# First expert's weight splits released by the last tile's logits, the routing slots and the first gathered rows

## The chip, the cores and the metric

The kernel runs on one core of one Trainium2 chip. The metric is the device time of one execution in microseconds (us); less is better. The engines of the core are named as the profile names them: PE is TensorE (matmuls), PEld its weight loads, DVE is VectorE, ACT is ScalarE, POOL is GpSimd and SP is SyncE, which here only issues transfers.

## The reference

The reference is a stack of four layers over 1024 tokens of width 1024. The change touches the feed-forward part of the first two layers, an expert-choice mixture with 16 experts:

```python
def expert_choice_ffn(xn, w_router, w_gate, w_up, w_down):
    cap = EC_CAPACITY_FACTOR * T // N_EXPERTS            # 128 tokens per expert
    aff = jax.nn.softmax((xn @ w_router).astype(jnp.float32), axis=-1)
    g, idx = lax.top_k(jnp.swapaxes(aff, 1, 2), cap)     # every expert picks its tokens
    xg = xn[bidx, idx]
    hid = jax.nn.silu(jnp.einsum('becd,edf->becf', xg, w_gate)) * jnp.einsum('becd,edf->becf', xg, w_up)
    y = jnp.einsum('becf,efd->becd', hid, w_down) * g[..., None].astype(xn.dtype)
    return jnp.zeros_like(xn).at[bidx, idx].add(y)
```

Here T is 1024, D is 1024 and the inner width is 768, so w_gate and w_up of one expert are 1024 x 768 and w_down is 768 x 1024.

## The kernel before

Every matmul in full precision is done in three products. An operand is split into a high part (rounded by ACT) and a low part (the rest, mostly by DVE), and high x low, low x high and high x high are added up on PE. So each weight that is loaded costs ACT one pass and DVE (or POOL) one pass before PE can use it.

The class `Moe` holds one feed-forward part. `mix_out` walks over eight tiles of 128 tokens: PE projects, `route_tile` adds the residual, normalizes, and makes the router's logits. ACT copies the logits out of PSUM as `lgs` (L1047), and for the last tile (t = 7) this is the last thing ACT has to do before the routing. `route` then finds each expert's 128 best tokens with a long row of small DVE instructions, and ends with `slot`: for each token its place in each expert's list. `slz` (L1165) is a column of zeros made from `slot`.

`experts` loops over the 16 experts. `fetch(e)` makes a one-hot map `oh` from `slot` on DVE (L1216), multiplies it on PE to get the list of token numbers (`idx`), casts it on DVE (L1223), sums the gains on DVE (`gsc`, L1231), and gathers the 128 rows `xg` with an indirect transfer that POOL issues (L1233). The map has one buffer, so the next expert's map waits for the matmuls of the one before. `tokens(e)` transposes the rows on PE (`xgT`) and splits them into `xgh` (ACT) and `xgl` (DVE); for the first expert in pieces of 128 x 256. The experts' `fetch(0)` and `fetch(1)` stand ahead of the loop, `fetch(e + 2)` and `tokens(e + 1)` inside it with raised priority.

`load` brings one unit of weights, 128 x 3072 (1536 KB): half of a gate, up or down matrix. SP issues it (L1186), and it is split in three stretches of 1024 columns. Units are counted in `self.units`: units 1 and 2 are the first expert's gate, 3 and 4 its up, 5 and 6 the second expert's gate, 7 and 8 its up, and then 9 and 10 the first expert's down (an expert's down follows the next expert's gate and up). Raw weights have four buffers for gate/up/down and two more, high and low parts have three buffers each; a load into a buffer waits for the low parts made from the unit that was in it.

Units 1 to 4 are loaded long before the routing ends. Units 1 to 3 are split by two lines of their own, L1195 and L1196: the high part adds `slz`, which is zero, as its bias, so that it waits for the slots. From unit 4 on, `K.split` (L130 on ACT, L134 on DVE or POOL) does it.

The order of instructions on each engine is fixed when the kernel is built: a planner runs through the kernel on a simulated timeline and puts an instruction on its engine's queue by priority and by the time at which its inputs are there. On the chip each engine then takes its queue strictly in order.

Of the kernel before, what the change touches and what calls it, by code (L numbers as in the profile page):

```python
# [10 lines left out]
F32 = mybir.dt.float32  # L11
# [3 lines left out]
AF = mybir.ActivationFunctionType  # L15
OP = mybir.AluOpType
# [4 lines left out]
P = 128  # L21
T = 1024
D = 1024
NT = T // P
KT = D // P
# [905 lines left out]
class Moe:  # L931
# [5 lines left out]
    def prepare(self, pool):  # L937
        K, nc, a = self.K, self.K.nc, self.K.a
        self.rt = pool.tile([P, KT, 32], F32, name="rt")
        nc.gpsimd.memset(self.rt, 0.0)  # L940
        nc.sync.dma_start(out=self.rt[:, :, 0:NE], in_=a["router_w"][self.layer].rearrange("(k p) e -> p k e", p=P))
        gc = K.small.tile([KT, P], F32, name="rgr", tag="colraw", bufs=2)
        nc.sync.dma_start(out=gc, in_=a["ffn_norm_g"][self.layer].rearrange("(k p) -> k p", p=P))
        gt = K.psum("rgt", "mm")
        K.transpose(gt[:, 0:KT], gc)
        nc.vector.tensor_tensor(out=self.rt[:, :, 0:NE], in0=gt[:, 0:KT].rearrange("p (k o) -> p k o", o=1).broadcast_to([P, KT, NE]),
                                in1=self.rt[:, :, 0:NE], op=OP.mult)
        self.aff = pool.tile([P, NT, NE], F32, name="aff")
        self.rhs = pool.tile([P, NT, NE, 5], BF16, name="lrhs")
        with K.pool("iot", 1) as ip:  # L950
            iot = ip.tile([P, 2, NT, NE], F32, name="iot")
            nc.gpsimd.iota(iot[:, 0], pattern=[[0, NT], [0, NE]], base=0, channel_multiplier=1, allow_small_or_imprecise_dtypes=True)
            nc.gpsimd.iota(iot[:, 1], pattern=[[P, NT], [0, NE]], base=0, channel_multiplier=0, allow_small_or_imprecise_dtypes=True)
            nc.gpsimd.tensor_copy(out=self.rhs[:, :, :, 0], in_=iot[:, 0])
            nc.gpsimd.tensor_copy(out=self.rhs[:, :, :, 4], in_=iot[:, 1])
        self.iota = pool.tile([P, P], F32, name="iotac")
        nc.gpsimd.iota(self.iota, pattern=[[1, P]], base=-1000, channel_multiplier=0, allow_small_or_imprecise_dtypes=True)
        self.affp = pool.tile([P, 4, 2, 2, 32], F32, name="affp")
        nc.gpsimd.memset(self.affp, 0.0)
# [53 lines left out]
    def route_tile(self, wk, h, t, project):  # L1013

        K, nc = self.K, self.K.nc
        V = nc.vector
        ts = slice(t * P, (t + 1) * P)
        cuts = (0, 512, 1024) if t == NT - 1 else (0, 1024)  # L1020
        xn = wk.tile([P, D], F32, name="xn", tag="xn")
        xt = wk.tile([P, D], F32, name="xnt", tag="xnt")
        n = len(cuts) - 1
        ss = self.sp.tile([P, n], F32, name="ss", tag=f"rss{n}", bufs=2)
        out, tp = K.psum("out"), K.psum("xnT", "tp")
        if t % 2 == 0:
            self.e = self.sp.tile([P, 2, NE], F32, name="re", tag="re", bufs=2)
        ps = K.psum("lg", "mm")
        for i, (c0, c1) in enumerate(zip(cuts, cuts[1:])):
            cs = slice(c0, c1)  # L1030
            project(out, c0, c1)
            V.tensor_tensor(out=h[:, cs], in0=out[:, cs], in1=h[:, cs], op=OP.add)
            K.norm_stats(h[:, cs], xn[:, cs], ss[:, i:i + 1])
            for k in range(c0 // P, c1 // P):
                K.transpose(tp[:, k * P:(k + 1) * P], h[:, k * P:(k + 1) * P])
            nc.scalar.activation(out=xt[:, cs], in_=tp[:, cs], func=AF.Copy)
            for k in range(c0 // P, c1 // P):
                j = k % 4 * 32
                K.mm(ps[j:j + 32, 0:P], self.rt[:, k], xt[:, k * P:(k + 1) * P], k < 4, k >= 4)
        nc.sync.dma_start(out=self.hD[ts, :], in_=h)  # L1040
        if n > 1:
            V.tensor_tensor(out=ss[:, 0:1], in0=ss[:, 0:1], in1=ss[:, 1:2], op=OP.add)
        ss = ss[:, 0:1]
        V.tensor_scalar(out=ss, in0=ss, scalar1=1.0 / D, scalar2=EPS, op0=OP.mult, op1=OP.add)
        rs = K.rsqrt(ss, 1)
        ls = self.sp.tile([P, P], F32, name="lgs", tag="lgs", bufs=2)
        nc.scalar.activation(out=ls, in_=ps[:, 0:P], func=AF.Copy)  # L1047
        K.transpose(ps[:, P:2 * P], ls)
        lg = self.sp.tile([P, NE], F32, name="lg", tag="lg", bufs=2)
        V.tensor_reduce(out=lg, in_=ps[:, P:2 * P].rearrange("p (j e) -> p e j", j=4)[:, 0:NE], axis=AX.X, op=OP.add)  # L1050
        mx = self.sp.tile([P, 1], F32, name="rmx", tag="rmx", bufs=2)
        V.tensor_reduce(out=mx, in_=lg, axis=AX.X, op=OP.max)
        V.tensor_scalar(out=self.e[:, t % 2], in0=lg, scalar1=mx, scalar2=rs, op0=OP.subtract, op1=OP.mult)
        if t % 2:
            self.affinities(t - 1)

        def normed():
            V.scalar_tensor_tensor(out=xn, in0=h, scalar=rs, in1=self.gb, op0=OP.mult, op1=OP.mult)
            nc.sync.dma_start(out=self.xnD[ts, :], in_=xn)

        if t < NT - 1:
            normed()
        else:
            self.normed = normed
# [63 lines left out]
    def route(self, pool):  # L1128

        K, nc, tc, a = self.K, self.K.nc, self.K.tc, self.K.a  # L1130
        V = nc.vector
        aff = self.aff
        with K.pool(name="rt", bufs=1, side="right") as rp:
# [18 lines left out]
            for t in range(NT):  # L1152
                lo, n = t + 1, NT - t
# [3 lines left out]
            slot = pool.tile([P, NT, NE], F32, name="slot")  # L1157
# [3 lines left out]
            V.scalar_tensor_tensor(out=tmp, in0=tmp, scalar=-1000.0, in1=sel[:, 0:NT, 1], op0=OP.add, op1=OP.mult)  # L1161
            V.tensor_tensor(out=slot, in0=slot, in1=tmp, op=OP.add)
            self.slot = slot
            self.zero = pool.tile([P, 1], F32, name="slz")
            V.tensor_scalar(out=self.zero, in0=slot[:, 0, 0:1], scalar1=0.0, scalar2=None, op0=OP.mult)  # L1165

            rhs = self.rhs
            res = rp.tile([P, NT, NE], F32, name="affr")
# [10 lines left out]
    def load(self, W, k0, n, c):  # L1179


        K, nc = self.K, self.K.nc
        kt = W.shape[0] // P
        r3 = self.raw(n, c, self.units % 6 > 3)
        raw = r3.rearrange("p k c -> p (k c)")
        nc.sync.dma_start(out=r3, in_=W.rearrange("(p k) c -> p k c", k=kt)[:, k0:k0 + n, :])  # L1186
        hi = self.wp.tile([P, 3072], F32R, name="mwh", tag="mwh", bufs=3)
        lo = self.wp.tile([P, 3072], F32R, name="mwl", tag="mwl", bufs=3)
        self.units += 1
        for j in range(3):  # L1190
            s = slice(j * 1024, (j + 1) * 1024)
            if self.units > 3:
                K.split(hi[:, s], lo[:, s], raw[:, s], lo_eng="pool" if self.units % 6 == 3 else "dve")
            else:
                nc.scalar.activation(out=hi[:, s], in_=raw[:, s], func=AF.Identity, bias=self.zero)  # L1195
                nc.vector.tensor_tensor(out=lo[:, s], in0=raw[:, s], in1=hi[:, s].bitcast(F32), op=OP.subtract)  # L1196
        return hi.rearrange("p (k c) -> p k c", k=n), lo.rearrange("p (k c) -> p k c", k=n)

    def accumulate(self, ps, parts, xh, xl, W, c):
# [48 lines left out]
    def experts(self, x0):  # L1248

        K, nc, a, L = self.K, self.K.nc, self.K.a, self.layer  # L1250
        V = nc.vector
        self.units, self.first = 0, []
        with K.pool("exw", 1) as self.wp, K.pool("exr2", 2) as self.rawp2, K.pool("ex", 2) as wk, K.pool("exx", 2, side="right") as xk:
            ahead = [self.fetch(wk, xk, 0), self.fetch(wk, xk, 1)]
            x = self.tokens(xk, ahead[0], 2)
            last = None
            for e in range(NE):
                idx, g, _ = ahead[e]
# [6 lines left out]
                for name in ("gate", "up"):  # L1265
# [3 lines left out]
                    if name == "gate" and e + 1 < NE:  # L1269
                        with K.first():  # L1270
                            x = self.tokens(xk, ahead[e + 1])
# [42 lines left out]
class Gqa:  # L1314
# [60 lines left out]
    def project(self, u, ws, wk, uh, ul, t):  # L1375

        K, nc = self.K, self.K.nc
        ts = slice(t * P, (t + 1) * P)
        ps = K.psum("qk")
        for j, (wh, wl) in enumerate(ws):  # L1380
            K.mm3(ps[:, j * 256:(j + 1) * 256], lambda k: uh[:, k, ts], lambda k: ul[:, k, ts], lambda k: wh[:, k], lambda k: wl[:, k], KT, n=256)
        if u == 1:
            p3 = ps[:, 0:256].rearrange("p (h d) -> p h d", h=4)
            K.split(self.v[:, t, :, 0:64], self.v[:, t, :, 64:128], p3)
            return
        x = self.rotated(wk, ps, u, t)
        tp = K.psum("qkT")
        for b in range(4):
            K.transpose(tp[:, b * P:(b + 1) * P], x[:, b * P:(b + 1) * P])
        tv = tp.rearrange("p (b t) -> p b t", b=4)  # L1390
        o, nq = (2, 4) if u else (0, 2)
        nc.scalar.activation(out=self.qT[:, o:o + nq, ts], in_=tv[:, 0:nq], func=AF.Copy, scale=0.125)
        if u == 0:
            nc.scalar.activation(out=self.kT[:, :, ts], in_=tv[:, 2:4], func=AF.Copy)
# [962 lines left out]
```

## Time and profile before

| what | value |
|---|---|
| time, median of 3 runs | 3875.89 us |
| lowest and highest | 3873.57, 3886.39 us |
| time of the profiled execution | 3871.14 us |
| its span | 3869.4 us |
| PE busy | 3548.5 us (92%) |
| DVE busy | 2800.8 us (72%) |
| ACT busy | 2089.2 us (54%) |
| POOL busy | 1068.8 us (28%) |

The span runs from the first to the last instruction of the profiled execution; its own time lies 1.7 us above. The slots are there at 932 us of the span in the first layer and at 2066 us in the second, and the expert loops follow. The places that the change touches are short: some 40 us from the last tile's logits to the second expert's first matmul, once in each layer, so they are read from the timeline of each engine and not from sums over the span.

### The profile page before, as it was taken

The page shows a single profiled execution, that of the slowest core. Times are in us where ns is not written, and L with a number is a line of the kernel's source. Part 1 is how long each engine was busy: PE and PEld are TensorE (multiplying, and loading weights), DVE is VectorE, ACT ScalarE, POOL GpSimd, SP SyncE. Part 2 cuts the span into 40 slices and gives each one's busy share as a digit, 9 for nine tenths or more (in the row PEclk, how much of TensorE's full clock was granted, in tenths as well). Part 3 has the DMA queues.
Part 4 walks back from the last instruction along what each step waited for, and adds up shares of the span by engine and source line. Part 5 has one row for each costly group of instructions (what it writes and reads, how often), then busy time and mean ns, then how long its engine had stood idle before and what let it go on. Part 6 is the DMA issues. An engine that isn't in the chain of part 4 may idle for free. (4 is left out here: it accounts for less than half of the span.)

```text
span 3869.4 us, 52797 instructions
## 1 busy us (share of the span) xinstructions
PE 3548.5 (92%) x19679; PEld 3015.0 (78%) x19679; DVE 2800.8 (72%) x4844; ACT 2089.2 (54%) x3234; POOL 1068.8 (28%) x939
## 2 busy tenths in 40 slices
PE   7997999985999989899895999989998999999998
PEld 6885878764988879877785988878876877778777
DVE  6547878857988779777777988776476866666565
ACT  4333432222776763689834776754486138665520
POOL 2004655400454321244401454322343000000010
PEclk9998999987999999999997999999999999999999
DMA  4223233354999961000265999961113312222441
GB/s 155 96 83 108 104 133 129 125 198 170 355 357 350 357 237 41 16 12 10 61 225 203 372 352 355 356 199 44 48 32 100 121 43 96 85 96 66 142 144 63
DMA packets 221321, 603.64 MB, mean 156 GB/s; under 512 B 23350, under 2 KB 129704, under 8 KB 195465
## 3 DMA queue, kind: packets, MB, share of 16 engines
q1 hardware_dynamic: 209369, 558.59, 40.2%
q0 software_dynamic: 11696, 41.69, 4.1%
q8 instruction: 155, 2.54, 0.3%
q14 instruction: 101, 0.83, 0.1%
HBM read 503.60 MB, written 96.60 MB: 155 GB/s over the span
## 5 line engine op out<-in xcount | busy, mean ns | idle before, releaser
L134 DVE TENSOR_TENSOR mwl<-mwr,mwh 128x1024 fp32r<-128x1024 f32 x468 | 612.7, 1360 | 67.4 <-ACT mwh L130 66.5
L130 ACT ACTIVATE mwh<-mwr 128x1024 fp32r<-128x1024 f32 x558 | 545.5, 1050 | 55.6 <-PE up L176 29.3
L134 POOL TENSOR_TENSOR mwl<-mwr,mwh 128x1024 fp32r<-128x1024 f32 x90 | 252.7, 2836 | 295.9 <-ACT mwh L130 277.3
L1864 POOL DMA_DIRECT2D pyr<-y3T_d x31 | 23.5, 758 | 723.0 <-PE z L176 592.6
L1233 POOL DMA_INDIRECT xg<-xn_d,idx x32 | 69.5, 2173 | 414.4 <-ACT mwh L1195 281.5
L915 POOL TENSOR_TENSOR oh<-oh,oh 64x256 f32<-64x256 f32 (+1 forms) x56 | 55.2, 985 | 396.9 <-ACT oh L914 382.4
L176 PE MATMUL gate<-mwh,xgl 128*128 128x384 f32 x512 | 140.2, 355 | 8.8 <-DVE xgl L134 8.8
L176 PE MATMUL gate<-mwl,xgh 128*128 128x384 f32 x512 | 138.4, 348 | 1.0 <-DVE mwl L134 0.7
L134 DVE TENSOR_TENSOR gpl<-pT,gph 128x512 fp32r<-128x512 f32 x168 | 110.5, 684 | 39.6 <-ACT gph L130 25.7
L873 DVE TENSOR_REDUCE mx<-gs 128x1 f32<-128x1024 f32 x96 | 116.9, 1217 | 30.4 <-PE gs L176 30.1
L125 PE MATMUL pT<-ident,prob 128*128 128x128 f32 x896 | 125.7, 275 | 13.9 <-DVE gpl L134 8.3
L125 PEld LDWEIGHTS pT<-ident,prob 128*128 128x128 f32 x896 | 104.5, 141 | 39.8 <-ACT prob L875 7.1
L176 PE MATMUL gate<-mwh,xgh 128*128 128x384 f32 x512 | 135.0, 344 | 0.0
L176 PE MATMUL up<-mwl,xgh 128*128 128x384 f32 x512 | 133.3, 340 | 1.8 <-DVE mwl L134 1.8
L176 PE MATMUL up<-mwh,xgh 128*128 128x384 f32 x512 | 133.5, 340 | 0.0
L176 PE MATMUL up<-mwh,xgl 128*128 128x384 f32 x512 | 132.8, 340 | 0.0
L176 PE MATMUL out<-pwh,pyl 128*128 128x512 f32 x384 | 121.8, 398 | 10.0 <-DVE pyl L134 10.0
L176 PE MATMUL down<-mwl,hh 128*128 128x512 f32 x384 | 123.5, 403 | 3.0 <-POOL mwl L134 2.7
L176 PE MATMUL down<-mwh,hl 128*128 128x512 f32 x384 | 122.8, 399 | 0.0
L176 PE MATMUL out<-pwl,pyh 128*128 128x512 f32 x384 | 121.7, 398 | 0.0
L176 PE MATMUL out<-pwh,pyh 128*128 128x512 f32 x384 | 121.6, 398 | 0.0
L176 PE MATMUL down<-mwh,hh 128*128 128x512 f32 x384 | 121.2, 396 | 0.0
(746 smaller groups left out, 11329.1 us busy)
## 6 DMA issues: line engine op xcount, KB each, us to landing
mwr<-in_exp_w_gate_dram SPq DMA_DIRECT2D x64, 1536.0 KB
mwr<-in_exp_w_up_dram SPq DMA_DIRECT2D x64, 1536.0 KB
mwr<-in_exp_w_down_dram SPq DMA_DIRECT2D x64, 1536.0 KB
raw<-in_ssd_w_in_dram SPq DMA_DIRECT2D x40, 512.0 KB
csr<-cs_d SPq DMA_DIRECT2D x32, 512.0 KB
k_d<-kev SPq DMA_DIRECT2D x54, 256.0 KB
kt<-k_d SPq DMA_DIRECT2D x54, 256.0 KB
raw<-in_hy_w_in_dram SPq DMA_DIRECT2D x10, 1024.0 KB
```

What stands on the lines that cost most here:

```text
L125: self.nc.tensor.transpose(out, in_, self.ident[:n, :n])
L130: nc.scalar.activation(out=hi, in_=src, func=AF.Copy)
L134: e.tensor_tensor(out=lo, in0=src, in1=hi.bitcast(F32), op=OP.subtract)
L176: self.nc.tensor.matmul(out=out, lhsT=lhsT, rhs=rhs, start=start, stop=stop)
L873: nc.vector.tensor_reduce(out=mx, in_=ps, axis=AX.X, op=OP.max, negate=True)
L915: nc.gpsimd.tensor_tensor(out=o2, in0=o2, in1=o, op=OP.add)
L1233: nc.gpsimd.indirect_dma_start(out=xg, out_offset=None, in_=self.xnD, in_offset=bass.IndirectOffsetOnAxis(ap=idx[:, 0:1], axis=0))
L1864: K.nc.gpsimd.dma_start(out=raw, in_=yT[q].rearrange("(p k) t -> p k t", k=self.kt)[:, :, t * P:(t + 1) * P])
```

## The change

The high parts of units 1 to 3 no longer take their zero from the slots. `route_tile` makes a new zero `lgz` on ACT from the last tile's `lgs`, and that is now the bias. The low parts of these units become a three-operand instruction on DVE, (raw + zero) - high, whose zero is a column: for unit 1 the zero from the slots, for units 2 and 3 a new zero `xgz`, which DVE makes from the last low part of the first expert's rows after `tokens` (whose last piece is written last). All these zeros have the value 0, so no result changes.

```diff
@@ prepare
         self.aff = pool.tile([P, NT, NE], F32, name="aff")
+        self.zero = pool.tile([P, 1], F32, name="lgz")
@@ route_tile
         nc.scalar.activation(out=ls, in_=ps[:, 0:P], func=AF.Copy)
+        if t == NT - 1:
+            nc.scalar.activation(out=self.zero, in_=ls[:, 0:1], func=AF.Copy, scale=0.0)
@@ route
-            self.zero = pool.tile([P, 1], F32, name="slz")
-            V.tensor_scalar(out=self.zero, in0=slot[:, 0, 0:1], scalar1=0.0, scalar2=None, op0=OP.mult)
+            self.late = [pool.tile([P, 1], F32, name=n) for n in ("slz", "xgz")]
+            V.tensor_scalar(out=self.late[0], in0=slot[:, 0, 0:1], scalar1=0.0, scalar2=None, op0=OP.mult)
@@ load
                 nc.scalar.activation(out=hi[:, s], in_=raw[:, s], func=AF.Identity, bias=self.zero)
-                nc.vector.tensor_tensor(out=lo[:, s], in0=raw[:, s], in1=hi[:, s].bitcast(F32), op=OP.subtract)
+                nc.vector.scalar_tensor_tensor(out=lo[:, s], in0=raw[:, s], scalar=self.late[self.units > 1], in1=hi[:, s].bitcast(F32), op0=OP.add, op1=OP.subtract)
@@ experts
             x = self.tokens(xk, ahead[0], 2)
+            V.tensor_scalar(out=self.late[1], in0=x[1][:, KT - 1, 0:1].bitcast(F32), scalar1=0.0, scalar2=None, op0=OP.mult)
```

## Rows read from the trace of the kernel before

**Rows 1.** Timeline of ACT, first layer: start, busy us, instruction, idle before and releaser

```profile
904.25 0.28 ACT L1047 ACTIVATE lgs<-lg 128x128 f32<-128x128 f32 x1 [0.61 <-PE lg L176]
914.50 0.56 ACT L1171 ACTIVATE lrhs<-aff 128x128 bf16<-128x128 f32 x1 [9.97 <-DVE aff L1078]
...
932.63 9.47 ACT L1195 ACTIVATE mwh<-mwr,slz 128x1024 fp32r<-128x1024 f32 x9 [15.45 <-DVE slz L1165]
942.06 0.38 ACT L130 ACTIVATE xgh<-xgT 128x256 fp32r<-128x256 f32 x1
```

**Rows 2.** Timeline of DVE, first layer, slots to first rows

```profile
932.44 0.15 DVE L1165 TENSOR_SCALAR slz<-slot 128x1 f32<-128x1 f32 x1
932.51 1.22 DVE L1216 TENSOR_TENSOR oh<-iotac,slot 128x1024 bf16<-128x1024 f32 x1
933.81 1.23 DVE L1196 TENSOR_TENSOR mwl<-mwr,mwh 128x1024 fp32r<-128x1024 f32 x1
934.95 0.15 DVE L1223 CAST idx<-idx 128x1 int32<-128x1 f32 x1
...
936.22 3.49 DVE L1196 TENSOR_TENSOR mwl<-mwr,mwh 128x1024 fp32r<-128x1024 f32 x3
...
940.76 0.15 DVE L1223 CAST idx<-idx 128x1 int32<-128x1 f32 x1
...
940.89 5.76 DVE L1196 TENSOR_TENSOR mwl<-mwr,mwh 128x1024 fp32r<-128x1024 f32 x5
946.57 1.63 DVE L134 TENSOR_TENSOR xgl<-xgT,xgh 128x256 fp32r<-128x256 f32 x4
```

**Rows 3.** Timeline of PE, first layer

```profile
936.36 0.58 PE L176 MATMUL idx<-lrhs,oh 128*128 128x4 bf16 x16 [1.99 <-DVE oh L1216]
940.88 1.94 PE L125 MATMUL xgT<-ident,xg 128*128 128x128 f32 x8 [3.94 <-DMA xg<-xn_d,idx]
947.04 1.01 PE L176 MATMUL gate<-mwh,xgl 128*128 128x384 f32 x2 [4.22 <-DVE xgl L134]
...
956.42 0.74 PE L125 MATMUL xgT<-ident,xg 128*128 128x128 f32 x4 [3.66 <-DMA xg<-xn_d,idx]
...
972.17 0.51 PE L176 MATMUL gate<-mwh,xgl 128*128 128x384 f32 x2
```

**Rows 4.** Timeline of POOL, first layer

```profile
936.06 1.32 POOL L1233 DMA_INDIRECT xg<-xn_d,idx  x1 [141.63 <-ACT mwh L1195]
941.20 6.31 POOL L1233 DMA_INDIRECT xg<-xn_d,idx  x1 [3.82 <-DVE gsc L1231]
```

**Rows 5.** Timeline of SP's queue, first layer

```profile
938.60 5.00 SPq L1186 DMA_DIRECT2D mwr<-in_exp_w_up_dram  x2
```

**Rows 6.** Stretches: PE, PEld, DVE, ACT, POOL busy (x), clock, DMA share, GB/s

```profile
956.90:960.20 3.30, 3.30 (x13) 3.30 (x13) 0.69 (x1) 0.60 (x1) 0.00 (x0) 0.50 0.25 94
...
972.00:977.00 5.00, 5.00 (x30) 5.00 (x30) 5.00 (x6) 3.44 (x5) 0.00 (x0) 1.00 0.89 317
957.50:965.00 7.50, 7.50 (x38) 7.50 (x38) 3.75 (x4) 4.44 (x6) 0.00 (x0) 0.81 0.04 15
```

**Rows 7.** Instructions of L1058, all: min/median/max ns

```profile
L1058 DVE SCALAR_TENSOR_TENSOR xn<-hres,rs_y,ffn_gb x16: 1266/1278/1285, 819.5 to 2040.1; 128x1024 f32<-128x1024 f32 x16
```

**Rows 8.** Transfers by queue, 953 to 956 us: packets, MB, share

```profile
q0 software_dynamic: 107, 0.37, 41.1%
q1 hardware_dynamic: 50, 0.44, 34.8%
```

**Rows 9.** Transfers by queue, 941 to 944 us

```profile
q1 hardware_dynamic: 83, 1.02, 91.1%
```

**Rows 10.** Timeline of PE, second layer

```profile
2080.26 1.01 PE L176 MATMUL gate<-mwh,xgl 128*128 128x384 f32 x2 [4.58 <-DVE xgl L134]
...
2105.58 0.51 PE L176 MATMUL gate<-mwh,xgl 128*128 128x384 f32 x2
...
2247.02 0.93 PE L125 MATMUL hT<-ident,hid 128*128 128x128 f32 x3 [2.10 <-DVE xgl L134]
```

## Prediction

> **What bounds the kernel now.** The page gives PE 92% of the span, so a change is worth something only where PE stands still or runs at its lower clock. I read the timeline of ACT first, then DVE, PE, POOL and SP around the slots, then stretches for the clock, then the same places in the second layer.
>
> ACT copies the last logits at 904.25, does nothing until 914.50, and after short copies waits 15.45 us for the zero from the slots; only then does it make nine high parts in 9.47 us [rows 1]. DVE is the engine that ends last here: after the slots it has three one-hot maps of 1.22 us, nine low parts at some 1.16 us each, and the casts between them, without a pause until 946.57 [rows 2]. The first expert's rows are on the chip at 940.88, when PE transposes them, but the first low part of the rows is made at 946.57, behind five low parts of weights, and the first gate matmul starts at 947.04 after PE has stood 4.22 us [rows 2, 3]. So the weights' low parts, needed later, sit in front of the rows' low parts, needed first.
>
> A second stop follows: PE waits 3.66 us until 956.42 for the second expert's rows [rows 3]. That gather is issued late (941.20), since its cast comes at 940.76 although its matmuls, begun at 936.36, take 0.58 us; and POOL needs 6.31 us for it where the first took 1.32 [rows 2 to 4]. After the stop PE's granted clock is 0.50, the 1.2 GHz level, for some 3.3 us; later it is 1.00 [rows 6]. The second expert's gate begins at 972.17 straight behind the first expert's up, 25.13 us after the first gate matmul [rows 3]. The second layer has the same picture: 2080.26 to 2105.58 is 25.32 us [rows 10].
>
> **The change part by part**, per layer, on the first layer's clock.
>
> *lgz and the early high parts.* One tiny ACT instruction; nearest row 0.28 us [rows 1], taken as 0.2. High parts would run from about 904.75 to 914.25, in the gap that ends at 914.50 [rows 1]. Cost nothing: the cover is ACT's idle time. If they ran over, the copy at 914.50 and then its readers on DVE would be late; the margin is 0.25 us, and 0 to 0.3 us is the bound. Gain by itself nothing either: high parts are not what ends last. ACT is free when the rows come.
>
> *Three-operand low parts.* The nearest row of that form and size is 1.28 us against 1.22 [rows 2, 7]: 0.06 more each, 0.2 us for the three of unit 1 and 0.4 for the other six. Below nothing it cannot be, as it does the same elements with one more operand.
>
> *xgz.* One column, as slz: 0.15 us [rows 2]. It holds up the six low parts of units 2 and 3 on DVE's queue. Behind them stand the third expert's cast, the second expert's rows and the low parts of unit 4. PE wants unit 2 only after 24 matmuls and unit 3 after 48.
>
> *Unit 1's low parts come before the first cast.* Their high parts are now ready when the slots are, so all three are free to go at the same moment as the first map. What the planner then does is seen in before: behind the second map it queued the three low parts that were ready, and the second expert's cast, whose matmuls end at about 936.94, came only at 940.76 [rows 2, 3]. I take the same for the first expert: map 932.51 to 933.7, three low parts at 1.2 us, cast at 937.35 instead of 934.95. That is 2.4 us lost: the gather goes out at 938.45 instead of 936.06 [rows 4]. The other end is 0 lost (cast after one low part, as before).
>
> *The first gather then meets a load.* SP issues the next load when unit 1's last low part is done: before at 938.60, 2.5 us behind the gather [rows 4, 5]; now at about 937.4, ahead of it. Without a collision the rows land at 940.88 + 2.4 = 943.3. If the gather were served only after the whole load (1.57 MB at 1.02 MB in 3 us is 4.6 us [rows 9], of which 1 us has passed), it lands 3.6 us later, at 946.9. In between: when a gather and a load were in flight together they moved 0.37 and 0.44 MB in 3 us, near equal shares [rows 8]; 0.52 MB in about 4.2 us instead of 2.2 is 2 us more, landing 945.3. I take this, the only row that shows both queues at work together.
>
> The Trainium skill, page "DMA: Bandwidth & Descriptors", section "Queues, rings and completion order", says an engine takes turns between queues but finishes a whole packet of one before it turns. If a load's share on an engine is one packet, the gather waits for the load, which is the later end above and would make the sum 6.2 instead of 9.4 us; it speaks against the change.
>
> *Rows to gate.* Transposes 940.88 to 942.06, one high part 0.38, low part to first matmul 0.47 [rows 1 to 3], with a hand-off 2.1 us. First gate matmul at 945.3 + 2.1 = 947.4 against 947.04 (945.4 and 949.0 at the ends). So the wait that is removed is filled again by the later cast and the load.
>
> *The second stop goes.* With units 2 and 3 held back, DVE's queue is short when the second expert's matmuls end: second map 937.5 to 938.7, matmuls to 939.3, third map to 940.5, cast at 940.6, much as before, but then no low parts run beside POOL and no second load is out until unit 2 is split. At 4.82 us from issue to landing, as the first gather had [rows 3, 4], the rows are there at 946, at 949 behind the first gather and its load; PE asks for them some 6 us after its first gate matmul, past 953. So 3.66 us of waiting go, and with them the second stretch at 1.2 GHz. Its price: 13 matmuls in 3.30 us against 30 in 5.00 [rows 6] is 1.1 us; half of 3.3, if all depended on the clock, 1.65; I take 1.4. From first gate to second gate 25.13 - 3.66 - 1.4 = 20.1 us.
>
> *What is late next.* Unit 2's low parts start at about 949.3, unit 3's end at 956.7. PE reaches unit 2 after 13 matmuls in 3.3 us, 11 at 5/30 us [rows 6], one list of 0.58 and transposes of 0.74 us [rows 3], some 6.4 us behind 947.4, and unit 3 after 24 more, 4 us later; the first low part of each is made at 950.5 and 954.1: both hidden, with 3 us to spare. The next two loads go out at about 953 and 957 instead of 943 and 947; the transfers stand nearly still from 957.5 to 965 (0.04 busy) [rows 6], which takes up the 9 us. Without that gap the loads would be late by some 1.5 us.
>
> *Sum.* Second gate at 947.4 + 20.1 = 967.5 instead of 972.17: 4.7 us a layer, 9.4 us for two. Before's execution took 3871.14 (span 3869.4 and 1.7 around it), so 3861.7; the median of the runs shown lies 4.75 above that execution, so 3866.5 against 3875.89.
>
> **The rivals.**
>
> *The cast stays early* (the planner takes it after one low part). For: that was so before for the first expert. Against: there only one low part was ready. First gate at 943.0, second at 963.1: 9.1 a layer, 3857.7.
>
> *The gather waits for the whole load.* For: the second gather took 15.2 us with loads out [rows 3, 4]. Against: the equal shares. First gate 949.0, second 969.1: 3.1 a layer, 3869.7. The page of the Trainium skill named above describes this case.
>
> *The second stop stays*, because the second gather is held again. For: 6.31 us on POOL end 0.86 us after the five low parts on DVE end [rows 2, 4]. Against: those low parts now come later. First gate 947.4, then 25.13: 0.4 lost a layer, 3876.6: the change would not do what it does on paper.
>
> *Slower.* The first gather fares as the second did, 15.2 us from issue to landing [rows 3, 4]: landing 953.7, first gate 955.8, second 975.9: 3.7 lost a layer, 3883.3. It decides from a landing after 950.0, where the gain is used up; against it: only one load can be out, since the others wait for low parts that wait for these rows.
>
> Later stops of PE, as the 2.10 us at 2247 [rows 10], may fall otherwise when the queue order shifts; each is worth 2 to 4 us in each layer, either way.
>
> **How the numbers follow.** Chances: forecast 0.47, early cast 0.15, gather behind the load 0.14, second stop stays 0.08, slower 0.07, later stops re-dealt beyond these 0.09 (0.04 better, 0.05 worse). The prediction is the forecast's 3866. The range 3853 to 3884 holds early cast and slower rival, and leaves some 2 in 10 outside with the later stops. About 0.3% (11.6 us) can be told from no change here. The forecast's own range 3859 to 3871 crosses 3864.3, with some 0.42 below. Faster: 0.20 of the forecast, 0.14 early cast, 0.02 behind the load, 0.04 rest: 0.40. Slower by as much: 0.02 of the slower rival, 0.01 of the stop that stays, 0.05 rest: 0.08. Within: 0.52.
>
> **What would show it.** Right: nine high parts on ACT by 914.3; cast of the first list near 937.3; first gate matmul near 947; no wait on `xgT` near 953; second gate near 967.5; the same in the second layer. Wrong: a first cast near 935; rows landing after 950; lrhs late on ACT; or PE stops elsewhere in the expert loops that differ from before's.

## The result and the profile after

The kernel after took 3852.36 us (median of 6 runs, 3846.49 to 3856.18) against 3878.61 for the kernel before (6 runs): ratio 0.9933, interval 0.9922 to 0.9944, so 26.2 us less where 9.4 were forecast. The profiled execution has a span of 3844.8 us instead of 3869.4; it was the shortest of the six.

The queues of all engines are the same up to `lgz`, yet the profiled execution of after is already 3.64 us earlier there (`lgs` at 900.61, before 904.25 [rows 1]). That need not come from the change: in two more executions of the same kernel (e7 and e12 below) `lgs` comes at 907.04 and 906.49. Times of after below are read 3.64 us earlier than the prediction's clock. ACT of after, first layer (start, busy us, instruction):

```profile
900.92 0.20 ACT L1050 ACTIVATE lgz<-lgs 128x1 f32<-128x1 f32 x1
901.15 9.46 ACT L1200 ACTIVATE mwh<-mwr,lgz 128x1024 fp32r<-128x1024 f32 x9
910.87 0.56 ACT L1174 ACTIVATE lrhs<-aff 128x128 bf16<-128x128 f32 x1 [0.26 <-DVE aff L1081]
```

The high parts fill the gap that ended with `lrhs` [rows 1], with 0.26 us to spare. DVE of after, against [rows 2]:

```profile
928.80 0.15 DVE L1168 TENSOR_SCALAR slz<-slot 128x1 f32<-128x1 f32 x1
...
930.00 3.67 DVE L1201 SCALAR_TENSOR_TENSOR mwl<-mwr,slz,mwh 128x1024 fp32r<-128x1024 f32 x3
933.59 0.15 DVE L1228 CAST idx<-idx 128x1 int32<-128x1 f32 x1
...
937.12 0.15 DVE L1228 CAST idx<-idx 128x1 int32<-128x1 f32 x1
...
943.29 0.42 DVE L134 TENSOR_TENSOR xgl<-xgT,xgh 128x256 fp32r<-128x256 f32 x1 [5.95 <-ACT xgh L130]
...
945.67 7.26 DVE L1201 SCALAR_TENSOR_TENSOR mwl<-mwr,xgz,mwh 128x1024 fp32r<-128x1024 f32 x6
```

Three low parts stand ahead of the first cast, as forecast; the rows' low parts no longer wait for weights; units 2 and 3 follow. POOL and SP's queue of after, against [rows 4, 5]:

```profile
934.70 1.32 POOL L1238 DMA_INDIRECT xg<-xn_d,idx  x1 [143.87 <-DVE gsc L1236]
937.56 0.99 POOL L1238 DMA_INDIRECT xg<-xn_d,idx  x1 [1.54 <-DVE gsc L1236]
```

```profile
933.74 16.01 SPq L1191 DMA_DIRECT2D mwr<-in_exp_w_up_dram  x2
953.01 5.55 SPq L1191 DMA_DIRECT2D mwr<-in_exp_w_down_dram  x2
```

The load goes out 0.96 us ahead of the first gather; the second gather takes 0.99 us on POOL instead of 6.31. What the transfer queues moved in after (q1 carries the load, q0 the gathers; packets, MB, share of 16 engines), from 936 to 938.9 us and then from 939.5 to 941.6:

```profile
q1 hardware_dynamic: 97, 1.19, 97.3%
```

```profile
q0 software_dynamic: 211, 0.80, 99.6%
q1 hardware_dynamic: 4, 0.00, 0.1%
```

The two do not share: the gather, issued at 934.70, moves nothing while the load runs. Its first packet starts at 938.99, 4.3 us behind its issue, where the load is all but through; in before, with no load ahead, the first packet came 2.0 us behind the issue (938.09). The second layer of after shows the same, 4.5 us (2061.89 behind 2057.40). PE of after, against [rows 3]:

```profile
941.75 1.95 PE L125 MATMUL xgT<-ident,xg 128*128 128x128 f32 x8 [6.16 <-DMA xg<-xn_d,idx]
943.77 1.01 PE L176 MATMUL gate<-mwh,xgl 128*128 128x384 f32 x2
...
947.97 0.69 PE L125 MATMUL xgT<-ident,xg 128*128 128x128 f32 x4
...
963.16 0.51 PE L176 MATMUL gate<-mwh,xgl 128*128 128x384 f32 x2
```

The second expert's transposes wait for nothing, and the second gate comes 19.39 us after the first gate instead of 25.13. So the place of the change comes out at the times forecast. The missing gain is farther on. These are the two expert loops, from the first gate matmul to the end of the last `down` (columns: stretch, length, then busy us of PE, PEld, DVE, ACT and POOL, clock, DMA share, GB/s), of before and of after:

```profile
947.04:1415.39 468.35, 450.68 (x2556) 415.89 (x2556) 377.51 (x362) 331.26 (x378) 190.94 (x75) 0.99 0.91 338
2080.26:2549.98 469.72, 450.34 (x2556) 416.18 (x2556) 376.67 (x360) 328.71 (x375) 194.96 (x75) 0.99 0.90 336
```

```profile
943.77:1403.24 459.47, 444.92 (x2556) 409.14 (x2556) 385.28 (x370) 331.93 (x379) 186.75 (x74) 0.99 0.92 344
2066.25:2523.48 457.23, 444.44 (x2556) 407.60 (x2556) 370.26 (x367) 328.30 (x376) 180.86 (x74) 0.99 0.93 346
```

The loops are 8.88 and 12.49 us shorter. With the 3.64 us before the change, 0.37 lost between `slz` and the first gate of the first layer, 1.8 won between the loops and 1.9 lost behind the second, this makes, but for rounding, the 24.6 us between the spans. What PE waited for in the second layer's loop (us in total, times, longest), before and after:

```profile
PE hT L125 <- DVE xgl L134: 5.4, 3, 2.1
...
PE xgT L125 <- DVE gsc L1231: 4.3, 3, 2.5
PE xgT L125 <- DMA xg<-xn_d,idx: 3.8, 1, 3.8
```

```profile
PE xgT L125 <- DVE gsc L1236: 3.1, 2, 2.5
...
PE hT L125 <- DVE xgl L134: 1.2, 1, 1.2
```

The stop of the second expert's rows (3.8) is gone, and so are two of the stops of 2.1 us at `hT`, far behind the edit; [rows 10] show one of them. PE's queue changed there too: the planner dealt the second loop anew. (`hT` are the transposes of an expert's hidden rows.) That belongs to the program and not to one execution: the 5.4 us at `hT` come again in e1, e5 and e6, which have the queues of before, and the 1.2 us in e9, which has those of after.

A third thing differs. Steady gate matmuls of after, 30 matmuls apart, are 5.20 us apart, 173 ns each; in before the gap from one start to the next is 177 ns (median over the gate and up matmuls of both loops; 173 in after). In before it repeats as some 174, 180, 175 and 178 ns, on average 176.6 at full clock against 173.4.

```profile
963.16 0.51 PE L176 MATMUL gate<-mwh,xgl 128*128 128x384 f32 x2
...
968.36 0.51 PE L176 MATMUL gate<-mwh,xgl 128*128 128x384 f32 x2
```

The new zeros take 64 bytes more beside the slots, which moves the gathered rows' tiles: `xgh` starts at byte 156864 of a partition in before and at 156800 in after. PE is 92% of the span and there are 3072 such matmuls.

### The profile page after: what moved, and what is told of

Its sections match the earlier page's. It is cut to its first block, busy times and chain, and to the rows that moved or that the text cites. A ratio compares the mean times of both kernels' runs of the same rounds, so it can differ in the third digit from the quotient of the medians.

```text
span 3844.8 us, 52790 instructions
## 1 busy us (share of the span) xinstructions
PE 3533.4 (92%) x19679; PEld 2995.6 (78%) x19679; DVE 2787.4 (72%) x4846; ACT 2089.7 (54%) x3236; POOL 1041.5 (27%) x939
## 4 chain that ended last, share of the span: by engine, by line
PE 62%; DVE 9%; ACT 5%; DMA 3%; issue 2%; POOL 1%; SPq 0%; ACTq 0%; DVEq 0%; POOLq 0%
PE out L176 12%; PE gate L176 8%; PE xbc L176 7%; PE up L176 6%; PE down L176 5%; PE z L176 3%; PE ov L176 2%; PE gs L176 2%; PE pT L125 2%; DVE mwl L134 2%; PE as L176 1%; PE qk L176 1%; PE yd L176 1%; PE xr L176 1%; PE mc L176 1%
## 5 line engine op out<-in xcount | busy, mean ns | idle before, releaser
L1870 POOL DMA_DIRECT2D pyr<-y3T_d x31 | 23.5, 760 | 726.1 <-PE z L176 592.3
L1238 POOL DMA_INDIRECT xg<-xn_d,idx x32 | 56.3, 1759 | 423.4 <-DVE gsc L1236 423.1
```

The costliest lines, as they stand in the source:

```text
L1238: nc.gpsimd.indirect_dma_start(out=xg, out_offset=None, in_=self.xnD, in_offset=bass.IndirectOffsetOnAxis(ap=idx[:, 0:1], axis=0))
L1870: K.nc.gpsimd.dma_start(out=raw, in_=yT[q].rearrange("(p k) t -> p k t", k=self.kt)[:, :, t * P:(t + 1) * P])
```

## The experiments

Kernels of one group ran on one chip beside the kernel before, whose median was 3869.95 (e1 to e4), 3873.29 (e5 to e8), 3877.84 (e9 to e11) and 3872.99 us (e12 to e14). Ratios are to that kernel, with the 95% interval in brackets.

**Place: e1, e10, e11 on the kernel before, e2 on the kernel after.** An unused tile, every queue unchanged:

```diff
             self.zero = pool.tile([P, 1], F32, name="slz")
+            pad = pool.tile([P, 16], F32, name="pad")    # e1, e10; e11: [P, 8]; e2: the same in after
```

> The kernel before with an unused tile of 64 bytes beside `slz`; every engine's queue stays as it was, only tiles on the right side of the on-chip memory move 64 bytes down, to where the kernel after has them (the first gathered rows' high parts from 156864 to 156800). Theory A (the gate and up matmuls run at another pitch because `xgh` and `xgl` lie elsewhere): median gap between gate/up matmuls 173 ns instead of 177, some 3 ns x 3072 matmuls = 9 to 10 us less, ratio to before near 0.9975, all of it in the two expert loops. Rival B (the shorter pitch of the kernel after comes from its other queue order or transfers): gap stays 177 ns, ratio 1.000.

> e1 once more, as a second draw. Theory A2: gaps of 173 ns again in both loops; the second gather on POOL takes either 6.31 us, with a second stop, or 1.77 us without one, as in the draws of before, so a loop is near 464 or near 460 us; ratio to before 0.997 to 0.999. Rival: gaps of 177 ns this time, ratio 1.000.

> The kernel before with an unused tile of 32 bytes: `xgh` at 156832, queues unchanged. No theory says which pitch this place has; by the kernels so far 156864 gave 177 ns, 156800 gave 173, 156736 gave 173 to 174. If it is 177 the rule is an address above some place, if 173 the first place is the odd one. With 177: ratio 1.000; with 173: 0.997 to 0.999.

> The kernel after with an unused tile of 64 bytes, queues unchanged; `xgh` moves on by 64 bytes, to 156736, which lies to 128 as in the kernel before (remainder 64). Theory A, with the remainder to 128 as what counts: gap back to 177 ns, 9 to 10 us more than after, ratio to before near 0.9957. Theory A with another period than 128: gap stays 173 ns, ratio as after. Rival B: gap 173 ns, ratio 0.993 as after.

e1 took 3866.89 us, ratio 0.9992 (0.9981 to 1.0002); e10 3869.81, 0.9983 (0.9975 to 0.9992); e11 3877.40, 1.0001 (0.9990 to 1.0011); e2 3852.37, 0.9957 (0.9942 to 0.9971). Medians of the gap: 173 ns in e1 and e10, 175 in e11's up matmuls (`xgh` at 156832), 173 to 174 in e2 (156736); e11 lies between its two cases. So the place sets the gap, with every queue unchanged, and the remainder to 128 is not the rule: e2 has the remainder of before and not its 177 ns. (The `down` matmuls, whose operands lie on the other side and do not move, stay at 227 to 228 ns in all kernels.) That e2's ratio is the 0.9957 that theory A put for 177 ns says nothing for it: e2 took what after took, and its group's before was faster. But the time of e1 and e10 is only 3 and 8 us less, by e1's interval perhaps nothing, and their loops differ from each other though the programs are the same. POOL of e1, then of e10, second gather of the first layer:

```profile
941.00 1.77 POOL L1234 DMA_INDIRECT xg<-xn_d,idx  x1 [3.81 <-DMA xg<-xn_d,idx]
```

```profile
938.98 6.31 POOL L1234 DMA_INDIRECT xg<-xn_d,idx  x1 [3.81 <-DVE gsc L1232]
```

With 1.77 us the second expert's rows come in time and the loop is 459.98 us; with 6.31 PE stops 3.66 us, the second gate comes 24.86 instead of 19.58 us behind the first, and the loop is 464.12. That was a draw (one program, and either value in different executions), not the pad, as the next two show.

**The kernel before, drawn again: e5 and e6.** No edit.

> The kernel before, unchanged, profiled once more. In e1, whose queues are those of the kernel before, the second gather took 1.77 us on POOL instead of 6.31, the second expert's rows came without a stop, and the gate/up matmuls ran 173 ns apart instead of 177; the two loops were 8.4 and 9.8 us shorter. Theory C (execution or chip, not the pad): this profile looks like e1: 1.77 us, no second stop, 173 ns, loops near 460 us, about 3857 to 3870 us. Theory D (the 64 bytes did it): 6.31 us, a second stop of 3.7 us in both layers, 177 ns, loops near 469 us.

> The same once more, as a second draw. Theory C: as e1, or between it and the first profile of before. Theory D: as the first profile of before.

One execution each, 3871.57 and 3869.66 us. Both keep 177 ns, so the gap belongs to the program, not to the execution. The gather is a draw: in e5, first and second layer,

```profile
940.84 6.32 POOL L1233 DMA_INDIRECT xg<-xn_d,idx  x1 [3.81 <-DVE gsc L1231]
```

```profile
2078.01 1.77 POOL L1233 DMA_INDIRECT xg<-xn_d,idx  x1 [3.97 <-DVE gsc L1231]
```

and the second loop, without the stop, is 466.67 us against 469.72 and 471.10 in the two draws with it. Over the six profiled executions with these queues, the second gather took 6.3 us in nine of twelve layers and 1.77 in three. With after's queues no low part runs beside it, and it took 0.97 to 0.99 in twelve layers of twelve (after, e2, e7, e9, e12, e13).

**The kernel after again, at the new place (e7, e12) and at the old (e9, e13).** e7 and e12 are unchanged. In e9 and e13 all queues are those of after, but `slz` and `xgz` lie in a pool of their own on the other side, so `xgh` is back at 156864 (lines shortened):

```diff
-            self.late = [pool.tile([P, 1], F32, name=n) for n in ("slz", "xgz")]
-            V.tensor_scalar(out=self.late[0], in0=slot[:, 0, 0:1], scalar1=0.0, scalar2=None, op0=OP.mult)
@@ experts
-        ..., K.pool("exx", 2, side="right") as xk:
+        ..., K.pool("exx", 2, side="right") as xk, K.pool("exz", 1) as self.zk:
+            zk = self.zk
+            self.late = [zk.tile([P, 1], F32, name=n) for n in ("slz", "xgz")]
+            V.tensor_scalar(out=self.late[0], in0=self.slot[:, 0, 0:1], scalar1=0.0, scalar2=None, op0=OP.mult)
```

> The kernel after, unchanged, on the same chip as the kernel before. Theory C: before varies from chip to chip while after stands at 3852, so here the ratio is nearer to 1 than 0.9933: about 0.9955, as e2's. Theory D: 0.993 again.

> The kernel after with every queue as it is, but `slz` and `xgz` in a pool on the left side, so that the gathered rows and their high and low parts lie where they lay in the kernel before (`xgh` at 156864). Theory A2 (the place of `xgh` and `xgl` sets the pitch; e2 showed that the remainder to 128 is not the rule): gaps back to 177 ns in both loops, loops 4 to 6 us longer each than after's 459 and 457, no second stop; ratio to before 0.997 to 0.998, which is near the 9.4 us forecast. Rival (the queues of after give the pitch, and e1's was something else): 173 ns, ratio 0.9948 as e7.

> The kernel after, unchanged, beside e13 on one chip. In the accounts of the loops (idle time of PE, half of the time at 0.50, and the rest), the rest is 440 to 441 us at 173 ns and 444 to 445 at 177 ns. Expected: loops near 459 and 457 us, falls of the clock near 160 us behind the first gate in the first layer and near 242 in the second, ratio to before 0.993 to 0.995.

> e9 once more. If the pitch is worth what the rest says, 3.7 us a loop, and the missing clock falls of e9 were a draw: falls appear, loops near 462 us, 5 to 8 us above e12. If the queues at 177 ns have fewer falls every time (a PE that is a little slower stands a little less): no fall behind the start again, loops at 459, within 2 us of e12.

e7 3853.40 us, 0.9948 (0.9936 to 0.9959); e9 3854.29, 0.9943 (0.9928 to 0.9957); on one chip e12 3851.85, 0.9950 (0.9935 to 0.9966), and e13 3854.45, 0.9958 (0.9943 to 0.9973). e7 lies nearer to theory C (0.9955) than to D (0.993): from group to group it is before whose time moves, not after's. The gap is 177 ns again at the old place (in e13 175 for the first layer's up matmuls, with the same average of 176.6); these two rows of e9 are 30 matmuls apart, 5.30 us:

```profile
964.99 0.52 PE L176 MATMUL gate<-mwh,xgl 128*128 128x384 f32 x2
...
970.29 0.51 PE L176 MATMUL gate<-mwh,xgl 128*128 128x384 f32 x2
```

So theory A2 was right on the gap and wrong on the time: e9's ratio is 0.9943, not 0.997 to 0.998. e13's median lies 2.6 us above e12's, which six and seven runs cannot tell from nothing, but the loops agree: those of e9 and e13 together take 2.6 us more, on average, than those of after, e7 and e12. An account of the loops shows why. Length less idle time of PE, less half of the time at a granted clock of 0.50 (from the trace's clock), leaves the rest (all in us):

| loop | length | PE idle | time at 0.50 | rest |
|---|---|---|---|---|
| before, first and second layer | 468.35, 469.72 | 17.67, 19.38 | 13.29, 13.30 | 444.0, 443.7 |
| after | 459.47, 457.23 | 14.55, 12.79 | 9.54, 6.63 | 440.2, 441.1 |
| e12 (as after) | 459.57, 457.40 | 14.43, 12.63 | 9.74, 6.43 | 440.3, 441.6 |
| e9 (after, old place) | 459.34, 458.89 | 13.29, 12.21 | 2.95, 2.95 | 444.6, 445.2 |
| e13 (the same) | 460.80, 458.97 | 13.32, 12.21 | 6.17, 3.12 | 444.4, 445.2 |

The longer gap costs some 4 us of the rest in each loop, but PE stands a little less and the clock falls less often. The account is rough: half of the time at 0.50 takes off too much where the clock fell often, as in the second loop of e3 below (27.4 us at 0.50, rest 435.0). The same stop of 2.10 us, in e12 and in e13, with what came behind it (PE, then the stretch behind it with its clock in the third column from the end):

```profile
1109.62 0.93 PE L125 MATMUL hT<-ident,hid 128*128 128x128 f32 x3 [2.10 <-DVE xgl L134]
1110.21 0.99 PE L176 MATMUL gate<-mwh,xgl 128*128 128x384 f32 x2
```

```profile
1109.40:1112.80 3.40, 3.17 (x11) 3.18 (x12) 3.40 (x5) 2.21 (x3) 1.19 (x1) 0.50 1.01 429
```

```profile
1105.42 0.67 PE L125 MATMUL hT<-ident,hid 128*128 128x128 f32 x3 [2.10 <-DVE xgl L134]
1105.85 0.60 PE L176 MATMUL gate<-mwh,xgl 128*128 128x384 f32 x2
```

```profile
1105.20:1108.60 3.40, 3.18 (x19) 3.18 (x20) 3.40 (x5) 2.21 (x3) 1.18 (x1) 1.00 1.00 424
```

In e12 PE starts 11 instructions at 1.2 GHz where in e13 it starts 19 at 2.4. It fell in after, e2, e7 and e12 and in neither e9 nor e13. Some 8.6 us earlier PE had stood 0.9 us in the four, for a low part from POOL, and 0.7 us in the two; what decides the fall stays open.

**One half alone: e3 and e8; the cast first: e4.** e3 leaves out `lgz` and lets the high parts wait for the slots; e8 lets all nine low parts wait for the slots; e4 is after with unit 1's zero made from the first expert's `gsc` (lines shortened; e3 also drops the two lines that make `lgz`):

```diff
e3 -                nc.scalar.activation(out=hi[:, s], in_=raw[:, s], func=AF.Identity, bias=self.zero)
e3 +                nc.scalar.activation(out=hi[:, s], in_=raw[:, s], func=AF.Identity, bias=self.late[0])
e8 -  ... scalar=self.late[self.units > 1] ...
e8 +  ... scalar=self.late[0] ...
e4 -            V.tensor_scalar(out=self.late[0], in0=slot[:, 0, 0:1], scalar1=0.0, scalar2=None, op0=OP.mult)
e4              ahead = [self.fetch(wk, xk, 0), self.fetch(wk, xk, 1)]
e4 +            V.tensor_scalar(out=self.late[0], in0=ahead[0][1], scalar1=0.0, scalar2=None, op0=OP.mult)
```

> Only the second half of the change: low parts of units 2 and 3 wait for the first expert's rows, the high parts wait for the slots as before. One low part then stands before the first cast, as in the kernel before, not three. Theory: the first cast at 2.5 us after `slz` instead of 4.8, first gather issued 3.6 us after it, rows landed near 8.5, first gate matmul near 10.7 us after `slz` (after: 15.0, before: 14.6), so some 4.3 us a layer better than after, ratio to before near 0.991. Rival: the early high parts matter and the second expert's rows are now late against the earlier first expert: the second stop of 3 to 4 us is back, ratio 0.993 to 0.995.

> Only the first half of the change: high parts early, but all nine low parts wait for the slots alone. All nine are then ready together, so the planner puts them ahead of the first cast: cast near 12.4 us behind `slot` (after 4.8, before 2.5), gather out 1.1 later, rows 7 us later near 20.5, first gate near 22.6 us instead of 14.6; no second stop. Theory: 8 us a layer later at the first gate, some 8 of a loop's length given back where before has them to give: ratio to before near 1.002 to 1.005. Rival (DVE is not what orders these): the cast stays early and the ratio is below 0.995.

> The change, but the zero of unit 1's low parts is made from the first expert's `gsc`, so the first cast stands before all low parts. Theory: first gather issued 2.4 us earlier than in e3's nearest row of after (near 2.7 us behind `slot`), no load beside it, rows landed near 7.5, first gate near 9.7 us behind `slot` instead of 15.0: some 5 us a layer better than after, ratio to before 0.990 to 0.991. Rival: the second expert's rows come too late for the earlier first expert, or later stops in the loops fall worse: ratio 0.993 or above.

e8 took 3873.54 us, 0.9997 (0.9988 to 1.0007). Its DVE and PE in the first layer:

```profile
937.29 10.85 DVE L1201 SCALAR_TENSOR_TENSOR mwl<-mwr,slz,mwh 128x1024 fp32r<-128x1024 f32 x9
948.05 0.15 DVE L1228 CAST idx<-idx 128x1 int32<-128x1 f32 x1
```

```profile
958.72 1.94 PE L125 MATMUL xgT<-ident,xg 128*128 128x128 f32 x8 [8.67 <-DMA xg<-xn_d,idx]
960.74 1.01 PE L176 MATMUL gate<-mwh,xgl 128*128 128x384 f32 x2
```

All nine low parts stand ahead of the cast. The first gate comes 24.7 and 23.4 us behind the slots, 10.0 and 8.8 later than before (8 expected), and the loops, 460.3 and 459.5 us, give it back, so the ratio of 1.002 to 1.005 that was expected did not come. Early high parts alone are worth nothing, and that with the new place of `xgh` and its 173 ns in the time.

e3 took 3859.84 us, 0.9973 (0.9961 to 0.9984), which neither theory expected. Its first gate is 10.6 and 10.5 us behind the slots, as expected and 4.4 and 4.2 better than after's, and no second stop is back; its first loop is 458.64 us; but its second loop is 469.13. DVE and PE there:

```profile
2273.75 5.75 DVE L134 TENSOR_TENSOR mwl<-mwr,mwh 128x1024 fp32r<-128x1024 f32 x5
2279.43 0.14 DVE L1226 CAST idx<-idx 128x1 int32<-128x1 f32 x1
...
2279.56 2.35 DVE L134 TENSOR_TENSOR mwl<-mwr,mwh 128x1024 fp32r<-128x1024 f32 x2
2281.83 1.28 DVE L134 TENSOR_TENSOR xgl<-xgT,xgh 128x512 fp32r<-128x512 f32 x2
```

```profile
2279.79 0.68 PE L125 MATMUL xgT<-ident,xg 128*128 128x128 f32 x4 [1.53 <-DVE gsc L1234]
...
2282.57 0.67 PE L125 MATMUL hT<-ident,hid 128*128 128x128 f32 x3 [2.09 <-DVE xgl L134]
```

It is what the change mends at the loop's start, low parts of weights queued ahead of the rows' cast and low parts, now in mid-loop, five times over: PE waits 10.7 us at `hT` in this loop, against 3.3 in its first, and its clock is at 0.50 for 27.4 us, against 3.8. The text of both loops is one and the same; only the planner's order differs. That is worth some 10 us in one layer.

e4 took 3838.82 us, 0.9921 (0.9907 to 0.9935), 13.5 us less than e2 on the same chip, the best version; 0.990 to 0.991 was expected, and the interval reaches from there to the rival's 0.993. Its DVE and PE:

```profile
932.54 0.16 DVE L1227 CAST idx<-idx 128x1 int32<-128x1 f32 x1 [0.69 <-PE idx L176]
...
934.00 3.68 DVE L1200 SCALAR_TENSOR_TENSOR mwl<-mwr,slz,mwh 128x1024 fp32r<-128x1024 f32 x3
```

```profile
938.31 1.95 PE L125 MATMUL xgT<-ident,xg 128*128 128x128 f32 x8 [3.77 <-DMA xg<-xn_d,idx]
940.34 1.01 PE L176 MATMUL gate<-mwh,xgl 128*128 128x384 f32 x2
```

First gate 9.7 us behind the slots in both layers, as expected, 10.3 us earlier than e2's in the two together; loops 455.5 and 455.7 us. There is no sign of the rival: the second expert's rows come without a stop.

**The edit in the first layer alone: e14.**

```diff
-  ... bias=self.zero) ... scalar=self.late[self.units > 1] ...
+  ... bias=self.zero if self.layer == 0 else self.late[0]) ... scalar=self.late[self.units > 1 and self.layer == 0] ...
```

> The edit takes effect in the first layer alone; the second layer's weights wait for the slots as before; tiles lie as in after, so 173 ns in both loops. Theory: first layer's loop as after's, 459 us; second layer's first gate 14.6 us behind `slot`, second gather beside five low parts, so 1.77 or 6.31 us on POOL, its loop 460 to 467 us with stops of 2.1 us at `hT`; ratio to before 0.995 to 0.997, between e1 and after. Rival (the first layer's edit alone re-deals the second loop to the better): second loop at 457.

3856.59 us, 0.9961 (0.9949 to 0.9973), 4.7 us above e12 on the same chip. The second loop is 460.5 us (e12 457.4), with a gather of 1.84 us on POOL and no second stop, and with 3.3 us at `hT` instead of before's 5.4. So the first layer's edit does shift the queues that follow, but no time is won by it: e1's second loop, with before's queues, the same place and a gather of 1.77 us, is 459.9 us. The 3.1 us to e12 need the second layer's own edit, and the rival's 457 is out.

## Why the prediction fell short

**Right, on the prediction's clock** (after's times plus 3.64): high parts 904.8 to 914.3; three low parts at 1.28 us each, 0.06 more than before's as forecast, then the cast at 937.2 (forecast 937.35); load out at 937.4; gather out 938.3 (938.45); low parts of units 2 and 3 from 949.3 to 956.6 (949.3 to 956.7); no wait for the second expert's rows, although PE asks for them 4.2 us behind its first gate matmul and not 6.

**Right by luck: the landing of the first rows.** Transposes start at 945.4 (landing 945.3) and the first gate at 947.4 (947.4), but not because load and gather took equal shares. The load went first and the gather waited for it: the rival's mechanism. The Trainium skill, "DMA: Bandwidth & Descriptors", section "Queues, rings and completion order", has an engine drain a whole packet of one queue before it turns to the next; the trace agrees with the prediction's reading of it, as the gather's first packet came when the load was all but through. The rival's price was too high. It put the rest of the load, 3.6 us, on top of the gather's whole time; but the gather needs 2.0 us from its issue to its first packet even alone, and these ran beside the load. From issue to transposes it took 7.05 us instead of 4.82, so 2.2 us were lost, near the 2 us that equal shares gave. The row of near equal shares [rows 8] was taken with more than one load out.

**Nearly right.** First to second gate: forecast 20.1 us, measured 19.4 in the first layer; 19.8 and 19.7 at the old place (e9, e13). The price of the second stop with its clock, 5.0 us a layer, was 5.3 and 4.9 between e10 and e1, the same program on two chips. But it is a price that before pays in most executions, not in all.

**Wrong: the sum.** It carried the 4.7 us at the second gate unchanged to the end and left everything behind it as it was; later stops stood beside it as a rival of 2 to 4 us in each layer, with 0.04 for the better. From three profiles each of before (loops 468.6 and 469.2 us on average; before, e5, e6) and of after (459.2 and 457.2; after, e7, e12), the loops gain 21.3 us. With the old place (e9 and e13: 460.1 and 458.9) they gain 18.7. Of these, first to second gate gave 5.6 us in the first layer (25.4 to 19.7) and 3.7 in the second (23.5 to 19.8, less than in the first because e5 had no second stop to lose there; two matmuls of the second gate, which the new queue puts ahead of the rest, are taken off): 9.4 us. The other 9.4, half of what the queues won, lie behind the second gate, 2.9 in the first layer and 6.5 in the second, in stops that went (two of 2.1 us at `hT` in the second loop) and in a clock that falls less often. The new place of `xgh` adds 2.6. The later stops were what the rival had named, and 2 to 4 us for each fits the two that went; its chance was too small to move the range. The prediction's own last sign of being wrong, stops elsewhere in the loops that differ from before's, is what came. I had the row of one of these stops [rows 10], which waits for the rows' low part just as the first gate does [rows 3], and did not ask which way other queues would push it. The place of the tiles was not thought of at all.

**What stays open.** The 26.2 us beside the change's first measurement against the 20 to 21 of e7 and e12: before's median differs by up to 8.7 us between groups of runs, after's by 1.6. Part of that may be the gather's draw; it was not counted over unprofiled runs. The 1.8 us between the loops and the 1.9 behind them were not tried.

## What to carry to other kernels

Where a planner deals the queues, the first place that a change mends is only the first: look for the same pattern (bulk work queued ahead of the short piece that the bottleneck waits for) through the whole loop, and give the better and the worse deal a real chance, since e3 lost more in one loop than it won at two first gates. Order within the mended place can matter nearly as much as the mending: e4 moved one zero and won another 13.5 us. A time that comes out as forecast does not show the mechanism: look at the packets or the queue, as at the first gather here. Before a change is judged, pad the kernel by the bytes that it adds: a tile that moves another is an edit too.

## What the runs showed of the hardware

- The place of the gathered rows' tiles, whose parts are the stationary operand, changes the gap between full-speed matmuls: 384 columns every 177 ns with `xgh` at 156864, 175 at 156832, 173 at 156800, 173 to 174 at 156736, with every queue unchanged. These tiles moved together, so which of them matters is not shown, and the rule behind it was not found.
- The same indirect gather beside the same five low parts on DVE took 6.31 us on POOL in nine cases and 1.77 in three. 6.31 ends 0.9 us behind the fifth low part, 1.77 the same behind the first; with none beside it, it took 0.99. The Trainium skill, "SBUF — State Buffer", section "Who interferes with whom", has a DVE instruction with two SBUF inputs contend with a GpSimd one that reads SBUF, through shared ports that one of them holds alone, with the order of issue deciding who blocks; the traces agree that POOL waits, and do not show what lets it in after one low part or only after five.
- A gather issued 1 us behind a load of 1.57 MB moved its first packet only when the load was all but through, 4.3 us behind its issue instead of 2.0.
- A stop of PE of 2.10 us was followed by a granted clock of 0.50 in one kernel and 1.00 in another whose queues are the same.
